# Moving the on-chip buffers of a two-layer decoder trunk to multiples of 1 KB

## The chip, the core and the metric

The kernel runs on one core of a Trainium2 chip. The metric is the device time of one execution in microseconds (us), as the median of several runs. Within a core, TensorE (PE) multiplies matrices, VectorE (DVE), ScalarE (ACT) and GpSimd (POOL) do elementwise work, and SyncE (SP) issues the transfers from the chip's main memory into SBUF, the on-chip memory of 128 partitions. A tile of SBUF is a range of bytes that is the same in every partition; its start is one address. A matmul on TensorE is two instructions: a weight load (LDWEIGHTS, shown as PEld), which reads the stationary operand of 128 columns, and the MATMUL (PE), which streams the moving operand past it, here mostly 256 columns of four bytes, into PSUM, the accumulator memory.

## The reference

Two layers on 256 tokens of width 2048, each a normalised input projection, a causal mixer, a gate and an output projection with a residual; a final RMS norm follows. All in float32.

```python
def reference(x, positions, layer_norm, mla_w_in, ..., swa_w_out, final_norm):
    for i in range(DEPTH):                       # DEPTH = 2
        h = rmsnorm(x, layer_norm[i])
        if i % 2 == 0:                           # latent attention, 16 heads, ranks 512
            y, gate = mla_mixer(h, positions, ...)
            w_out = mla_w_out[j]
        else:                                    # window 128, 32 query heads on 4 key heads, sinks
            y, gate = swa_mixer(h, positions, ...)
            w_out = swa_w_out[j]
        x = x + (y * jax.nn.silu(gate)) @ w_out
    return rmsnorm(x, final_norm)
```

## The kernel before

Activations lie transposed: 16 tiles of 128 channels by 256 tokens. Float32 values are multiplied as a rounded high part plus a low part: `hs` (layer input), `ys` (gated mixer output) and `lat` (the latent vectors `cq` and `ck`) hold the two parts side by side, 256 columns each, so a tile has 2,048 bytes per partition. Each weight piece of 1,024 columns arrives in a tile `wraw` (five buffers), ScalarE rounds it into `whi` (line 89) and VectorE writes the rest into `wlo` (line 90), four buffers each. A projection step is then three matmuls on one weight tile of 128 columns (512 bytes), written by `proj`: high weights by high input (line 250), high by low (251), low by high (252). `slab` runs eight such steps, half of the 16 that one output chunk needs.

The order is written out by hand in one function. First come the latent projections, chunk by chunk as the weights arrive. Then a loop over eight pairs of heads: queries (from `cq`), the previous pair's value products `mix` (lines 450 to 453), rotary parts, keys, values (520 to 522, where the weight piece is the moving operand and `ck` the stationary one), and four gate slabs, with the pair's scores (544 to 552) behind the first and the transposes of its probabilities (`turn`, lines 342 and 343) behind the third. The output projection of this layer follows (32 slabs on `ys`), then keys and values of the second layer. Its loop over 16 pairs of heads has, in each round, a query slab, transposes, scores (642 to 645), the second query slab, a gate slab, the value products (670 to 672) and the second gate slab. The output projection of this layer ends the kernel, its last two chunks in another order (lines 728 and 735) so that the final norm can begin early.

Tiles come from pools. A pool is one stretch of SBUF, and its tiles lie one behind the other in the order in which the code first asks for them, each rounded up to 32 bytes; the pools lie one behind the other in the order in which they are opened: `const` (everything that lives for long, with small columns such as norm factors in between), `wpool` (`wraw`, `whi`, `wlo`) and `work` (temporaries, among them small columns of 8 or 16 bytes and the three probability tiles `p`). Each small tile so shifts all that stand behind it. Adding up the sizes gives these starts, in bytes past a multiple of 512; a piece of `whi` or `wlo` is read in steps of 512 bytes and the low half of `hs` lies 1,024 behind the high half, so that the remainder holds for every matmul on the tile:

| tile | read in | before | after |
|---|---|---|---|
| `hs`, `ys`, `cq`, `ck` | projections | 96 | 0 |
| `whi`, `wlo` | projections | 416 | 0 |
| `k1s`, `vs`, `krs` | scores, values | 96 | 0 |
| `qs`, `qh`, `ql` | scores | 416 | 0 |
| `kk`, `vh`, `vl` | scores, values | 480 | 0 |
| `pth`, `ptl`, `p` | values, transposes | 160 | 0 |
| `ident` | transposes | 32 | 352 |

Modulo 1,024, the pieces of `whi` and `wlo` start at 928 and 416 by turns before, at 0 and 512 after.

Of the kernel before, what the change touches and what calls it, by code (L numbers as in the profile page):

```python
# [18 lines left out]
F32 = mybir.dt.float32  # L19
# [6 lines left out]
P = 128  # L26
D = 2048
S = 256
# [10 lines left out]
QH, KVH, HD = 32, 4, 64  # L39
# [60 lines left out]
def trunk(ctx: ExitStack, tc: tile.TileContext, a: dict):  # L100
# [3 lines left out]
    const = ctx.enter_context(tc.tile_pool(name="const", bufs=1))  # L104
    wpool = ctx.enter_context(tc.tile_pool(name="wpool", bufs=1))
    work = ctx.enter_context(tc.tile_pool(name="work", bufs=2))
    ps_p = ctx.enter_context(tc.tile_pool(name="ps_p", bufs=3, space=PSUM))
    ps_s = ctx.enter_context(tc.tile_pool(name="ps_s", bufs=2, space=PSUM))
    ps_t = ctx.enter_context(tc.tile_pool(name="ps_t", bufs=1, space=PSUM))
# [25 lines left out]
        w.add(a["w_o1"][c], D)  # L135


    first = const.tile([P, 1], F32, name="first")
    dve.memset(first, 0.0)
    act.activation(out=first, in_=first, func=AF.Sin)  # L140


    w.load(1)
    gains = const.tile([P, 3 * KC + 2 * RC], F32, name="gains")
    nc.sync.dma_start(out=gains, in_=a["gains"])
    g0, g1, gf = gains[:, 0:KC], gains[:, KC:2 * KC], gains[:, 2 * KC:3 * KC]
    gq, gkv = gains[:, 3 * KC:3 * KC + RC], gains[:, 3 * KC + RC:]
# [2 lines left out]
    def xc(c):  # L150
        return x_t[c // XQ][:, c % XQ, :]

    for j in range(XQ):
        nc.sync.dma_start(out=xc(j), in_=a["x"][0][:, j, :])
        w.load(j + 2)
    freqs = const.tile([P, 4], F32, name="freqs")
    pos_i = work.tile([P, S], I32, tag="ro3", name="pos_i")
    sinks = const.tile([P, QH], F32, name="sinks")


    ident = const.tile([P, P], F32, name="ident")
    make_identity(nc, ident)

    fold = const.tile([P, P], F32, name="fold")
    pool.memset(fold, 0.0)
    for b in (0, ROPE, -ROPE):
        pool.affine_select(out=fold, in_=fold, compare_op=ALU.not_equal, fill=1.0, base=b,
                           pattern=[[-1, P]], channel_multiplier=1)
    ones = const.tile([P, 2], F32, name="ones")
    pool.memset(ones, 1.0)  # L170
    mhalf = const.tile([P, 2], F32, name="mhalf")
    pool.memset(mhalf, -0.5)

    mask_c = const.tile([P, 2 * P], F32, name="mask_c")
    mask_w = const.tile([P, 2 * P], F32, name="mask_w")
    pool.memset(mask_c, 0.0)
    pool.memset(mask_w, 0.0)
    for m in (mask_c, mask_w):
# [8 lines left out]


    def tiny(name, n=2, bufs=2):
        return work.tile([P, n], F32, tag=name, name=name, bufs=bufs)  # L190

    def split(dst, src):

# [31 lines left out]
    def rsqrt(name, tot, n, times=None):  # L225

        e = tiny("rs_e")
        if times is None:
            dve.tensor_scalar(out=e, in0=tot, scalar1=1.0 / n, scalar2=EPS, op0=ALU.mult, op1=ALU.add)
        else:  # L230
            dve.tensor_tensor(out=e, in0=tot, in1=times, op=ALU.mult)
            dve.tensor_tensor(out=e, in0=e, in1=times, op=ALU.mult)
            dve.tensor_scalar(out=e, in0=e, scalar1=1.0 / n, scalar2=EPS, op0=ALU.mult, op1=ALU.add)
        r = const.tile([P, 2], F32, name=name)
        pool.tensor_tensor(out=r, in0=e, in1=mhalf, op=ALU.pow)
        return r

# [24 lines left out]
    def bank(pool_, tag):  # L262
        return pool_.tile([P, 512], F32, tag=tag, name=tag)
# [48 lines left out]

    def softmax(ps, j, nm, sm, mask, scale, sink):

        p = work.tile([P, 3 * P], F32, tag="p", name="p", bufs=3)
        for i in range(2):
            cols = slice(0, P) if i == 0 else slice(P, 3 * P)
            src = ps[:, 0:P] if i == 0 else ps[:, S:2 * S]
            m = mask
            if i == 0:  # L320
                m = p[:, cols]
                dve.tensor_tensor(out=m, in0=ps[:, P:S], in1=mask[:, P:], op=ALU.add)
            c = 2 * i + j
            dve.tensor_tensor_reduce(out=p[:, cols], in0=src, in1=m,  # L324
                                     scale=scale if isinstance(scale, float) else scale[:, i:i + 1],
                                     scalar=BIG if sink is None else sink, op0=ALU.add, op1=ALU.min,
                                     accum_out=nm[:, c:c + 1])
            act.activation(out=p[:, cols], in_=p[:, cols], func=AF.Exp, scale=-1.0, bias=nm[:, c:c + 1],  # L328
                           accum_out=sm[:, c:c + 1])
        return p  # L330
# [55 lines left out]
    for k in range(KC):  # L386
        if k in (1, 3, 6):
            i = (1, 3, 6).index(k) + 1
            nc.sync.dma_start(out=x_t[i], in_=a["x"][i])
        if k == 3:  # L390
            nc.sync.dma_start(out=freqs, in_=a["freqs"])
            nc.sync.dma_start(out=pos_i, in_=a["pos"].partition_broadcast(P))
            nc.sync.dma_start(out=sinks, in_=a["sinks"].partition_broadcast(P))
        split_scaled(hs[k], xc(k), g0[:, k:k + 1])
        if k == 0:
            for half in range(2):
                hi, lo = w.next()
                for ws, x in ((hi, 0), (hi, 1), (lo, 0)):
                    for c in range(RC):
                        mm(acc[half * RC + c], lhsT=ws[:, c * P:(c + 1) * P], rhs=hs[0][:, x, :],  # L400
                           start=False, stop=False)
        elif k < KC - 2:
            hi, lo = w.next()
            for c in range(2 * RC):
                n = slice(c * P, (c + 1) * P)
                proj(acc[c], (hi[:, n], lo[:, n]), hs[k], False, False)
            sq_x.add(xc(k - 1))
        elif k == KC - 1:
            last = [w.next(), w.next()]
            for j in range(KC - 3, KC):  # L410
                sq_x.add(xc(j))
            for c in range(2 * RC):
                n = slice(c * P, (c + 1) * P)
                for j, (hi, lo) in enumerate(last):
                    proj(acc[c], (hi[:, n], lo[:, n]), hs[KC - 2 + j], False, j == 1 and c % 2 == 1)
                if c % 2 == 1:
                    finish(c - 1)
                    finish(c)
        if k == 6:
            pos_f = const.tile([P, S], F32, name="pos_f")  # L420
            dve.tensor_copy(out=pos_f, in_=pos_i)
            tables = {n: rope_tables(n, i, pos_f) for i, n in enumerate(("mla", "swa"))}
    cos0, sin0 = tables["mla"]
# [37 lines left out]
    for g in range(HEADS // 2):  # L461
# [18 lines left out]
        if g == 0:  # L480
            t = bank(ps_y, "yp")
            tot = [q.total(t[:, 4 * i:4 * i + 4]) for i, q in enumerate((sq_x, sq_c["q"], sq_c["k"]))]
            r0 = rsqrt("r0", tot[0], D)

            sqc = rsqrt("sqc", tot[1], RANK, r0)
            nsq = const.tile([P, 2], F32, name="nsq")
            dve.tensor_tensor(out=nsq, in0=sqc, in1=r0, op=ALU.mult)
            dve.tensor_scalar(out=nsq, in0=nsq, scalar1=-MLA_SCALE, scalar2=None, op0=ALU.mult)
            skc = rsqrt("skc", tot[2], RANK, r0)
            sk = const.tile([P, 2], F32, name="sk")  # L490
            dve.tensor_tensor(out=sk, in0=skc, in1=r0, op=ALU.mult)
            t = bank(ps_y, "yp")
            r0B = row("r0B", r0, t[:, 0:S])
            skB = row("skB", sk, t[:, S:])
            ps = bank(ps_s, "sc")[:, 0:S]
            mm(ps, lhsT=fold, rhs=krn, start=True, stop=True)
            kr = work.tile([P, S], F32, tag="ro3", name="ro3")
            rope(kr, ps, cos0, sin0, MASK_MLA)
            dve.tensor_tensor(out=kr, in0=kr, in1=r0B, op=ALU.mult)
            split(krs, kr)  # L500
# [14 lines left out]
        for i in range(2):  # L515
            t = slice(i * P, (i + 1) * P)
            for k in range(RC):
                n = slice(k * S, (k + 1) * S)
# [77 lines left out]
    for q in range(4):  # L596
        hi, lo = w.next()
        for i in range(2):
            t = slice(i * P, (i + 1) * P)
            for k in range(4):  # L600
                kk = 4 * q + k
                n = slice(k * S, (k + 1) * S)
# [6 lines left out]
        dve.scalar_tensor_tensor(out=vs[i][:, :, 1, :], in0=v, scalar=r1[:, i:i + 1],  # L609
                                 in1=vs[i][:, :, 0, :].bitcast(F32), op0=ALU.mult, op1=ALU.subtract)  # L610

    nsink = const.tile([P, QH], F32, name="nsink")
    dve.tensor_scalar(out=nsink, in0=sinks, scalar1=-1.0, scalar2=None, op0=ALU.mult)
    qs_of, sg_of, p_of, pt_of, y_of = {}, {}, {}, {}, {}

# [107 lines left out]
    for c in tail:  # L723
        last[c] = [w.next(), w.next()]
        ps = bank(ps_p, "pp")[:, 0:S]
        for k in range(KC):
            n = slice(k % (KC // 2) * P, (k % (KC // 2) + 1) * P)
# [3 lines left out]
    def chunk(c, t):  # L731
        ps = bank(ps_p, "pp")[:, 0:S].rearrange("p (a q) -> p a q", a=2)
        for k in range(KC):
            n = slice(k % (KC // 2) * P, (k % (KC // 2) + 1) * P)
            mm(ps, lhsT=last[c][k // (KC // 2)][0][:, n], rhs=ys[k][:, :, t], start=k == 0, stop=k == KC - 1)  # L735
        xl = xc(c)[:, t]
        for n in range(2):
            dve.tensor_tensor(out=xl, in0=ps[:, n, :], in1=xl, op=ALU.add)
        sq = work.tile([P, P], F32, tag=("hx", "yg")[c % 2], name="sql", bufs=2)
        act.activation(out=sq, in_=xl, func=AF.Square)  # L740
        return sq
# [28 lines left out]
    sq = chunk(KC - 2, t1)  # L770
    r2 = norm(t0, parts)
    parts = [sq, chunk(KC - 1, t1)]
    scaled(0, t0, r2)
    scaled(1, t1, norm(t1, parts))

# [80 lines left out]
```

## Time and profile before

| | |
|---|---|
| median of three runs | 680.67 us (680.66 to 681.06) |
| the profiled execution | 684.75 us, of which the span from first to last instruction is 683.0 |
| mean granted clock of TensorE | 0.996 |
| TensorE matmuls | 667.3 us busy, 5,718 instructions |
| VectorE, ScalarE, GpSimd | 532.2, 428.0 and 66.3 us busy |

Matmuls are pipelined: several are in flight at once, so a busy TensorE says little on its own. What one matmul costs in a full stream is the distance between its start and the next one's start. The 4.08 us between the profiled execution and the median are kept apart in what follows.

### The profile page before, as it was taken

To read this page: it belongs to the slowest core of one execution; us is meant where nothing else is said; L and a number is where in the kernel's file an instruction comes from. 1 tells how busy PE (TensorE), PEld (TensorE's weight loads), DVE (VectorE), ACT (ScalarE), POOL (GpSimd) and SP (SyncE) were. 2 spreads that over 40 slices of the span, in tenths; PEclk is the share of its full clock that TensorE was granted. 3 is DMA by queue.
4 is the path that set the end of the run, shared out by engine and by line. 5 is a ranking of instruction groups with operands and counts; after the bars stand their busy time and mean duration, and the time that the engine had idled before them with its cause. 6 is when DMAs were issued, how large, how long until landed. Compare 5 with 4: busy or idle time off the path is not lost.

```text
span 683.0 us, 14550 instructions
## 1 busy us (share of the span) xinstructions
PE 667.3 (98%) x5718; PEld 663.1 (97%) x5718; DVE 532.2 (78%) x1085; ACT 428.0 (63%) x853; POOL 66.3 (10%) x72
## 2 busy tenths in 40 slices
PE   8999999999999999999999999999999999999994
PEld 7999999999999999999999999999999999999994
DVE  5897787787688686666658899998998998766664
ACT  6667656666676665444446688788778778544430
POOL 3634000000000000111110000000000000022220
PEclk9999999999999999999999999999999999999998
DMA  8664454554554555555554545545445454455604
GB/s 311 252 206 168 161 161 144 185 167 144 183 162 150 174 167 174 196 183 189 184 187 160 180 141 169 166 147 177 160 157 158 157 177 158 156 188 195 204 32 124
DMA packets 37302, 117.00 MB, mean 171 GB/s; under 512 B 4209, under 2 KB 8945, under 8 KB 37233
## 3 DMA queue, kind: packets, MB, share of 16 engines
q1 hardware_dynamic: 37232, 116.06, 51.3%
q8 instruction: 45, 0.74, 0.4%
q14 instruction: 25, 0.20, 0.1%
HBM read 113.95 MB, written 2.10 MB: 170 GB/s over the span
## 4 chain that ended last, share of the span: by engine, by line
PE 88%; DVE 4%; ACT 3%; POOL 1%; issue 1%; DMA 1%; SPq 0%; DVEq 0%; ACTq 0%; POOLq 0%
PE pp L251 24%; PE pp L250 24%; PE pp L252 24%; PE pt L342 1%; DVE wlo L90 1%; ACT whi L89 1%; PE pp L735 1%; PE pp L520 1%; PE pp L522 1%; PE pp L521 1%; PE yp L670 1%; PE pt L343 1%; DVE x L762 1%; DMA wraw<-in_w_c 1%; PE sc L642 1%
## 5 line engine op out<-in xcount | busy, mean ns | idle before, releaser
L90 DVE TENSOR_TENSOR wlo<-wraw,whi 128x1024 fp32r<-128x1024 f32 (+1 forms) x217 | 259.9, 1199 | 88.6 <-ACT whi L89 87.0
L89 ACT CAST whi<-wraw 128x1024 fp32r<-128x1024 f32 (+1 forms) x217 | 222.9, 1029 | 168.7 <-PE pp L251 142.1
L252 PE MATMUL pp<-hs,wlo 128*128 128x256 f32 x860 | 239.6, 279 | 1.3 <-DVE wlo L90 1.2
L250 PE MATMUL pp<-hs,whi 128*128 128x256 f32 x860 | 240.4, 280 | 0.4 <-ACT whi L89 0.4
L251 PE MATMUL pp<-hs,whi 128*128 128x256 f32 x860 | 239.6, 279 | 0.5 <-DVE hs L200 0.5
L252 PEld LDWEIGHTS pp<-hs,wlo 128*128 128x128 f32 x860 | 161.5, 188 | 1.9 <-DVE wlo L90 1.9
L250 PEld LDWEIGHTS pp<-hs,whi 128*128 128x128 f32 x860 | 162.6, 189 | 0.6 <-ACT whi L89 0.6
L251 PEld LDWEIGHTS pp<-hs,whi 128*128 128x128 f32 x860 | 161.6, 188 | 0.9 <-DVE hs L200 0.9
L251 PE MATMUL pp<-ys,whi 128*128 128x256 f32 x480 | 133.9, 279 | 0.1
L250 PE MATMUL pp<-ys,whi 128*128 128x256 f32 x480 | 133.9, 279 | 0.0
L252 PE MATMUL pp<-ys,wlo 128*128 128x256 f32 x480 | 133.8, 279 | 0.0
L216 POOL TENSOR_TENSOR sq_x<-sq_x,sq 128x256 f32<-128x256 f32 x43 | 53.3, 1240 | 577.2 <-ACT sq L215 335.5
L250 PEld LDWEIGHTS pp<-ys,whi 128*128 128x128 f32 x480 | 91.2, 190 | 0.0
L251 PEld LDWEIGHTS pp<-ys,whi 128*128 128x128 f32 x480 | 90.1, 188 | 0.3 <-DVE ys L195 0.3
L252 PEld LDWEIGHTS pp<-ys,wlo 128*128 128x128 f32 x480 | 90.1, 188 | 0.0
L328 ACT ACTIVATE p<-p,nm 128x128 f32<-128x128 f32 x96 | 42.7, 446 | 15.3 <-DVE nm L324 15.3
L250 PE MATMUL pp<-cq,whi 128*128 128x256 f32 x96 | 27.3, 284 | 0.0
L200 DVE SCALAR_TENSOR_TENSOR hs<-x,gains,hs 128x256 fp32r<-128x256 f32 x32 | 24.9, 790 | 2.6 <-ACT hs L199 2.6
L252 PE MATMUL pp<-cq,wlo 128*128 128x256 f32 x96 | 26.7, 278 | 0.0
L251 PE MATMUL pp<-cq,whi 128*128 128x256 f32 x96 | 26.7, 278 | 0.0
L303 DVE TENSOR_TENSOR qs<-ro,qs 64x256 fp32r<-64x256 f32 x48 | 20.2, 421 | 7.5 <-ACT qs L302 6.3
L302 ACT CAST qs<-ro 64x256 fp32r<-64x256 f32 x48 | 19.2, 400 | 8.3 <-DVE ro L296 7.7
(242 smaller groups left out, 1133.6 us busy)
## 6 DMA issues: line engine op xcount, KB each, us to landing
wraw<-in_w_g SPq DMA_DIRECT2D x64, 512.0 KB, 3.7
wraw<-in_w_o SPq DMA_DIRECT2D x64, 512.0 KB, 3.5
wraw<-in_w_q SPq DMA_DIRECT2D x32, 512.0 KB, 3.6
wraw<-in_w_ukv SPq DMA_DIRECT2D x16, 512.0 KB, 3.5
wraw<-in_w_c SPq DMA_DIRECT2D x15, 512.0 KB, 6.7
wraw<-in_w_uq SPq DMA_DIRECT2D x8, 512.0 KB, 3.6
wraw<-in_w_uq SPq DMA_DIRECT2D x8, 256.0 KB, 2.6
wraw<-in_w_k SPq DMA_DIRECT2D x4, 512.0 KB, 3.4
```

Source lines behind the costliest of these rows:

```text
L89: self.nc.scalar.copy(out=hi, in_=src)
L90: self.nc.vector.tensor_tensor(out=lo, in0=src, in1=hi.bitcast(F32), op=ALU.subtract)
L200: dve.scalar_tensor_tensor(out=dst[:, 1, :], in0=src, scalar=col, in1=dst[:, 0, :].bitcast(F32), op0=ALU.mult, op1=ALU.subtract)
L216: pool.tensor_tensor(out=self.acc, in0=self.acc, in1=t, op=ALU.add)
L250: mm(ps, lhsT=wh, rhs=rhs[:, 0, :], start=first, stop=False)
L251: mm(ps, lhsT=wh, rhs=rhs[:, 1, :], start=False, stop=False)
L252: mm(ps, lhsT=wl, rhs=rhs[:, 0, :], start=False, stop=last)
L302: act.copy(out=dst[r, j, :], in_=src[r, :])
L303: dve.tensor_tensor(out=dst[o, j, :], in0=src[r, :], in1=dst[r, j, :].bitcast(F32), op=ALU.subtract)
L328: act.activation(out=p[:, cols], in_=p[:, cols], func=AF.Exp, scale=-1.0, bias=nm[:, c:c + 1], accum_out=sm[:, c:c + 1])
L342: nc.tensor.transpose(t[:, 0, j * S + i * P:j * S + (i + 1) * P], p[:, i * P:(i + 1) * P], ident)
L343: nc.tensor.transpose(t[:, 1, j * P:(j + 1) * P], p[:, 2 * P:3 * P], ident)
```

## The change

The number of tiles, their sizes, buffers, instructions, waits and the order on each engine stay as they are. Only where the tiles lie is different. The small columns leave `const` and `work` for a pool `small`, and the probability tiles leave `work` for a pool `probs`, both opened behind `work`. In `const`, the tiles that are not multiples of 1 KB are asked for first and together, so that `x` begins at 20,480 and `hs` at 36,864; a tile `rest` that nothing uses is added as the last one of `const`, and `wpool` begins at 131,072.

```diff
     work = ctx.enter_context(tc.tile_pool(name="work", bufs=2))
+    probs = ctx.enter_context(tc.tile_pool(name="probs", bufs=3))
+    small = ctx.enter_context(tc.tile_pool(name="small", bufs=1))
...
-    first = const.tile([P, 1], F32, name="first")
+    first = small.tile([P, 1], F32, name="first")
...
     gains = const.tile([P, 3 * KC + 2 * RC], F32, name="gains")
+    ident = const.tile([P, P], F32, name="ident")
+    sinks = const.tile([P, QH], F32, name="sinks")
+    freqs = const.tile([P, 4], F32, name="freqs")
+    mask_c = const.tile([P, 2 * P], F32, name="mask_c")
+    mask_w = const.tile([P, 2 * P], F32, name="mask_w")
+    pos_f = const.tile([P, S], F32, name="pos_f")
...
-    fold = const.tile([P, P], F32, name="fold")
+    fold = small.tile([P, P], F32, name="fold")
...
     def tiny(name, n=2, bufs=2):
-        return work.tile([P, n], F32, tag=name, name=name, bufs=bufs)
+        return small.tile([P, n], F32, tag=name, name=name, bufs=bufs)
...
-        r = const.tile([P, 2], F32, name=name)
+        r = small.tile([P, 2], F32, name=name)
...
-        p = work.tile([P, 3 * P], F32, tag="p", name="p", bufs=3)
+        p = probs.tile([P, 3 * P], F32, tag="p", name="p")
...
+    const.tile([P, S], F32, name="rest")
```

In the places left out, `ones`, `mhalf`, `nsq`, `sk` and `nsink` go to `small` in the same way, and the old lines of `freqs`, `sinks`, `ident`, `mask_c`, `mask_w` and `pos_f` are taken out.

More of the change, by code (lines that the diff above doesn't have):

```diff
@@ L155, in trunk @@
         w.load(j + 2)
-    freqs = const.tile([P, 4], F32, name="freqs")
     pos_i = work.tile([P, S], I32, tag="ro3", name="pos_i")
-    sinks = const.tile([P, QH], F32, name="sinks")
-    ident = const.tile([P, P], F32, name="ident")
     make_identity(nc, ident)
-    fold = const.tile([P, P], F32, name="fold")
+    fold = small.tile([P, P], F32, name="fold")
     pool.memset(fold, 0.0)
@@ L168, in trunk @@
                            pattern=[[-1, P]], channel_multiplier=1)
-    ones = const.tile([P, 2], F32, name="ones")
+    ones = small.tile([P, 2], F32, name="ones")
     pool.memset(ones, 1.0)
-    mhalf = const.tile([P, 2], F32, name="mhalf")
+    mhalf = small.tile([P, 2], F32, name="mhalf")
     pool.memset(mhalf, -0.5)
-    mask_c = const.tile([P, 2 * P], F32, name="mask_c")
-    mask_w = const.tile([P, 2 * P], F32, name="mask_w")
     pool.memset(mask_c, 0.0)
@@ L419, in trunk @@
         if k == 6:
-            pos_f = const.tile([P, S], F32, name="pos_f")
             dve.tensor_copy(out=pos_f, in_=pos_i)
@@ L485, in trunk @@
             sqc = rsqrt("sqc", tot[1], RANK, r0)
-            nsq = const.tile([P, 2], F32, name="nsq")
+            nsq = small.tile([P, 2], F32, name="nsq")
             dve.tensor_tensor(out=nsq, in0=sqc, in1=r0, op=ALU.mult)
@@ L489, in trunk @@
             skc = rsqrt("skc", tot[2], RANK, r0)
-            sk = const.tile([P, 2], F32, name="sk")
+            sk = small.tile([P, 2], F32, name="sk")
             dve.tensor_tensor(out=sk, in0=skc, in1=r0, op=ALU.mult)
@@ L610, in trunk @@
                                  in1=vs[i][:, :, 0, :].bitcast(F32), op0=ALU.mult, op1=ALU.subtract)
-    nsink = const.tile([P, QH], F32, name="nsink")
+    nsink = small.tile([P, QH], F32, name="nsink")
     dve.tensor_scalar(out=nsink, in0=sinks, scalar1=-1.0, scalar2=None, op0=ALU.mult)
```

## The prediction

> **What bounds the kernel now.** I read the page's shares first, then the chain that ended last, then what TensorE waited for.
>
> ```profile
> span 683.0 us, 14550 instructions
> ...
> PE 667.3 (98%) x5718; PEld 663.1 (97%) x5718; DVE 532.2 (78%) x1085; ACT 428.0 (63%) x853; POOL 66.3 (10%) x72
> ...
> PE 88%; DVE 4%; ACT 3%; POOL 1%; issue 1%; DMA 1%; SPq 0%; DVEq 0%; ACTq 0%; POOLq 0%
> PE pp L251 24%; PE pp L250 24%; PE pp L252 24%; PE pt L342 1%; DVE wlo L90 1%; ACT whi L89 1%; PE pp L735 1%; PE pp L520 1%; PE pp L522 1%; PE pp L521 1%; PE yp L670 1%; PE pt L343 1%; DVE x L762 1%; DMA wraw<-in_w_c 1%; PE sc L642 1%
> ```
>
> TensorE is busy 98% of the span, and the three matmuls of a projection step, lines 250 to 252, are 72% of the chain. The list of waits has next to nothing on TensorE; its longest is the first matmul of the warm-up:
>
> ```profile
> PE pp L385 <- DVE ys L382: 1.5, 1, 1.5
> ```
>
> So the time is the number of matmuls times the distance from the start of one to the start of the next. That distance isn't printed; it comes from the first and last start of one line's instructions in a stretch. Below are such rows for line 250, which issues every third matmul of a slab: two from the first output projection (260 to 347 us), two from the second (590 to 655), and one each from two neighbouring stretches of the sliding-window layer. Columns: count, duration min/median/max in ns, first and last start in us.
>
> ```profile
> L250 PE MATMUL pp<-ys,whi x247: 281/281/281, 259.9 to 346.8; 128*128 128x256 f32 x124
> L250 PEld LDWEIGHTS pp<-ys,whi x246: 192/192/192, 260.1 to 346.7; 128*128 128x128 f32 x123
> ...
> L250 PEld LDWEIGHTS pp<-ys,whi x192: 187/188/188, 589.9 to 654.8; 128*128 128x128 f32 x192
> L250 PE MATMUL pp<-ys,whi x192: 276/276/276, 590.0 to 654.9; 128*128 128x256 f32 x192
> ...
> L250 PE MATMUL pp<-hs,whi x16: 276/276/276, 401.4 to 406.5; 128*128 128x256 f32 x16
> ...
> L250 PE MATMUL pp<-hs,whi x16: 281/281/283, 407.6 to 412.9; 128*128 128x256 f32 x16
> ```
>
> The first stretch has 246 steps of three matmuls in 86.9 us: 353.3 ns a step, 117.8 ns a matmul. The second has 191 steps in 64.9 us: 339.8 ns, 113.3 a matmul. The same code on tiles at the same addresses has two paces, 4.5 ns (3.8%) apart. In the slow one the weight load of line 250 takes 192 ns in place of 188. The last two rows show both paces within 12 us of each other (15 steps in 5.1 and in 5.3 us).
>
> **What switches the pace.** I went through the sequence of all starts. Within a run of matmuls whose operands keep their starts modulo 512 bytes the pace never changes, however long the run. All 28 switches with three equal distances on either side lie within four matmuls of a change of these starts or of a gap. One place of each direction, from the timeline (start, duration):
>
> ```profile
> 446.38 0.28 PE L670 MATMUL yp<-pth,vs 128*128 128x256 f32 x1
> ...
> 446.83 0.28 PE L672 MATMUL yp<-ptl,vs 128*128 128x256 f32 x1
> 446.95 0.28 PE L250 MATMUL pp<-hs,whi 128*128 128x256 f32 x1
> ...
> 447.54 0.28 PE L252 MATMUL pp<-hs,wlo 128*128 128x256 f32 x1
> ```
>
> From 446.38 to 446.95 there are five distances (114 ns each), from 446.95 to 447.54 again five (118 ns). The step from the value products (moving operand 160 bytes past a multiple of 512, weights 96) to a slab (moving 96, weights 416) ends the fast pace, in all 16 such places. The other direction, from the value projection of the latent layer (moving 416, weights 96) to a gate slab:
>
> ```profile
> 144.71 0.28 PE L522 MATMUL pp<-whi,ck 128*128 128x256 f32 x1
> 144.83 0.28 PE L250 MATMUL pp<-hs,whi 128*128 128x256 f32 x1
> 144.95 0.28 PE L251 MATMUL pp<-hs,whi 128*128 128x256 f32 x1
> 145.07 0.28 PE L252 MATMUL pp<-hs,wlo 128*128 128x256 f32 x1
> ...
> 145.52 0.28 PE L250 MATMUL pp<-hs,whi 128*128 128x256 f32 x1
> ```
>
> Three distances of 120, then four in 0.45 us, 113 each. And a gap: after the last matmuls of a head pair's mix the next group starts slow.
>
> ```profile
> 137.68 0.36 PE L250 MATMUL pp<-cq,whi 128*128 128x256 f32 x1
> 137.88 0.28 PE L251 MATMUL pp<-cq,whi 128*128 128x256 f32 x1
> ...
> 138.35 0.28 PE L252 MATMUL pp<-cq,wlo 128*128 128x256 f32 x1
> ```
>
> One distance of 200 ns, then four in 0.47 us, 118 each. Of the matmuls of 256 columns, 2,735 distances are at the fast pace and 2,669 at the slow one, counted over the whole trace.
>
> **The change, part by part.** Instructions, waits and queue orders stay as they are, so no term comes from a moved step. Only addresses move.
>
> 1. Operands of the projections, and with them those of scores and values, now all start 0 bytes past a multiple of 512 (and of 1 KB but for a weight piece's odd columns). The changes of start that go with the switches above vanish, and the steady pair (96, 416) becomes (0, 0). No row of the trace has this pair, so the price is bounded from both sides. Best case inside what rows show: every slow distance becomes fast, 2,669 x 4.5 ns = 12.0 us less. By stage:
>
> ```profile
> 6.00:31.80 25.80, 23.85 (x196) 22.86 (x195) 20.46 (x32) 17.72 (x32) 12.88 (x11) 1.00 0.80 310
> 257.00:391.00 134.00, 133.76 (x1133) 133.30 (x1132) 92.76 (x135) 69.80 (x111) 16.57 (x16) 1.00 0.54 180
> 401.00:575.00 174.00, 174.00 (x1514) 174.00 (x1513) 161.05 (x413) 134.85 (x316) 0.00 (x0) 1.00 0.49 162
> ```
>
> (columns: stretch, its length, then busy time of PE, PEld, DVE, ACT, POOL; clock, DMA share, GB/s.) From 257 to 391 us nearly all is slow: 3.8% of 130 is 4.9. From 401 to 575, 6.6 of every 13.1 us are slow: 3.8% of 87 is 3.3. The latent layer's loop has 708 slow distances: 3.2. The first 32 us: 0.5. Sum 11.9, the 12.0 again. Worst case inside the rows: every fast distance becomes slow, 2,735 x 4.4 = 12.0 us more. I take three quarters of the gain, 9 us, and not all of it, because the gap row (137.68) shows that a gap can start the slow pace without any change of starts, and each head pair has such gaps.
>
> 2. TensorE reads across multiples of 1 KB less often. That alone I cost at nothing: weight pieces starting 416 past a multiple of 1 KB end before the next one, those starting 928 past it cross it, and the two alternate in every slab at one pace. A moving operand of two separate 512-byte runs (line 735) costs no more than one run of 1,024 bytes; this row of the chain gives 5.44 / 48 = 113.3 ns:
>
> ```profile
> 663.80 5.44 PE pp L735 x48
> ```
>
> 3. Vector, scalar and GpSimd operands and the landing places of transfers move too. Where TensorE sets the pace this is covered: in 401 to 575 us VectorE is the busiest other engine with 161.05 of 174.00. At the fast pace the stage still needs 170.7, so VectorE, at 94%, is late next but not yet the bound. Uncovered is the start: TensorE idles 25.80 - 23.85 = 1.95 us there, and VectorE works 20.46. A gain can be no more than the 1.95; a loss of 5% on VectorE's work would be 1.0. I take 0.
>
> Sum: the profiled execution took 684.75 us, 1.75 more than its span, and 4.08 more than the median of the runs, 680.67. 684.75 - 9 = 675.7; less the 4.08, 671.7, so 672. For this case alone 668.6 (all 12.0) to 677.
>
> **The rivals.**
>
> *Slower: the slow pace becomes the rule.* Place: the gate slab behind line 522, and the one behind the scores (line 552). There a change of start brings the fast pace back today; with equal starts nothing does until a gap that happens to end fast. Price: the fast part of the latent loop (787 distances x 4.4 ns = 3.5 us) and of the sliding-window layer (822: 3.6) make 7.1, so 688; with the second output projection (743: 3.3) and the start all 12.0, 692.7. It decides where more than half of the 5,404 distances end up slow. For it: gaps before a slab mostly end slow today. Against: the long stretch from 590 us is fast on the same addresses, so nothing in a slab itself brings the slow pace back.
>
> *Nothing changes: the paces have nothing to do with addresses.* The switches sit where the code goes from one kind of product to another, so the starts change together with the PSUM bank, the shape and the waits, and the trace can't part these. Then all switches stay: 680.7. Against: where the code goes from the scores' last product to a slab (line 645 to 250), bank and tiles change but not the starts modulo 512, and in all 14 such places the pace stays. [...]
>
> *One stage gains what another loses.* If gaps go on ending as they do now, the sliding-window layer is all fast (-3.3) and the latent loop all slow (+3.5): about 681.
>
> *More than the fast pace.* The uneven starts may have a part in the 113.3 ns too. The nearest rows with a weight load of the same 128 columns are transposes, with half the moving columns:
>
> ```profile
> 452.61 0.38 PE L342 MATMUL pt<-ident,p 128*128 128x128 f32 x2
> ...
> 453.15 0.27 PE L343 MATMUL pt<-ident,p 128*128 128x128 f32 x1
> ```
>
> Five distances in 0.54 us, 108 ns. If projections came to that, 12.0 + 5,404 x 5.3 ns = 40 us less on TensorE; VectorE's 161.05 would then hold the sliding-window stage, which keeps some 2: about 642. Against: those transposes also start 32 bytes off a multiple of 64, so a wrong start alone doesn't cost time there. [...]
>
> **How the numbers follow.** Fast pace nearly everywhere, 0.37; slow pace the rule, 0.26; nothing changes, 0.23; one stage against another, 0.05; more than the fast pace, 0.09. Faster by over 0.2% (1.4 us, about what a measurement of this kernel can tell from no change): 0.37 + 0.09 + 0.01 of the fifth = 0.47. Slower: 0.26 + 0.02 = 0.28. Within: 0.25. The likeliest case gives 672. The range leaves out the deep gain (0.09) and the end of the slow case in which all 12 us are lost (0.07): 666 to 691.
>
> **What would show it.** If right: line 250's rows in 260 to 347 us have 276 and 188 ns and 339.8 ns a step; the rows behind line 672 keep 113 ns; the sliding-window stage takes 171 us in place of 174. If the slow case: steps of 353.3 ns from 590 us on too. If addresses don't matter: the same switches at the same places. My forecast fails if the gaps set the pace alone, or if (0, 0) has a pace of its own, seen as a step that is neither 340 nor 353 ns.

## The result, and the profile after

The changed kernel takes 704.81 us (four runs, 704.57 to 705.25), the kernel before 680.66 in the runs beside it (680.48 to 681.06): 1.0355 times as long, 95% interval 1.0337 to 1.0373. The forecast was 672 with a range of 666 to 691. The profiled execution took 705.25 us, 20.5 more than that of before.

The page of the changed kernel:

```profile
span 703.5 us, 14550 instructions
...
PE 690.9 (98%) x5718; PEld 686.6 (98%) x5718; DVE 534.1 (76%) x1085; ACT 429.4 (61%) x853; POOL 66.3 (9%) x72
...
PE 89%; DVE 3%; ACT 3%; POOL 2%; issue 1%; DMA 1%; SPq 0%; DVEq 0%; ACTq 0%; POOLq 0%
...
L257 PE MATMUL pp<-hs,wlo 128*128 128x256 f32 x860 | 243.8, 284 | 1.2 <-DVE wlo L90 1.0
```

TensorE has 23.6 us more of busy time with the same 5,718 matmuls; VectorE, ScalarE and GpSimd have what they had, to 2 us (534.1, 429.4 and 66.3 against 532.2, 428.0 and 66.3). The rows of single instructions hardly betray it: the one of line 257 has 284 ns, its twin before had 279.

```profile
L252 PE MATMUL pp<-hs,wlo 128*128 128x256 f32 x860 | 239.6, 279 | 1.3 <-DVE wlo L90 1.2
```

The starts do. These are rows for the first matmul of a projection step, now line 255, in the two output projections (count, duration min/median/max in ns, first and last start in us):

```profile
L255 PEld LDWEIGHTS pp<-ys,whi x242: 188/192/192, 265.9 to 352.7; 128*128 128x128 f32 x121
L255 PE MATMUL pp<-ys,whi x242: 283/283/283, 266.0 to 352.8; 128*128 128x256 f32 x121
...
L255 PE MATMUL pp<-ys,whi x181: 279/283/283, 604.8 to 669.8; 128*128 128x256 f32 x181
```

The first holds 241 steps of three matmuls in 86.8 us, 360.2 ns a step; the second 180 in 65.0, 361.1 with a stop or two. Before, they had 353.3 and 339.8. So a step is neither of the two known, and a matmul costs 120.0 ns. That holds nearly everywhere: 5,156 of 5,403 distances between matmuls of 256 columns (those under 130 ns) lie between 119 and 121. Their mean went from 115.59 to 119.89 ns, which is 23.2 us; the 84 and 85 longer ones became 1.5 us shorter in sum, and the distances behind matmuls of other widths 0.1. That makes 21.5 us between the first matmul and the last (the parts are rounded); what lies outside of them became 1.0 us shorter, and the span grew by 20.5.

The places where the pace used to switch have no switch any more. Here is the step from the value products to a gate slab, in the timeline after:

```profile
459.09 0.28 PE L676 MATMUL yp<-ptl,vs 128*128 128x256 f32 x1
459.21 0.28 PE L255 MATMUL pp<-hs,whi 128*128 128x256 f32 x1
459.33 0.28 PE L256 MATMUL pp<-hs,whi 128*128 128x256 f32 x1
459.45 0.28 PE L257 MATMUL pp<-hs,wlo 128*128 128x256 f32 x1
...
461.13 0.28 PE L256 MATMUL pp<-hs,whi 128*128 128x256 f32 x1
```

Every distance is 0.12 us, ahead of the slab and in it.

### The profile page after: what moved, and what is told of

Same layout as the page of the kernel before. It is cut to its first block, busy times and chain, and to the rows that moved or that the text cites. A ratio compares the mean times of both kernels' runs of the same rounds, so it can differ in the third digit from the quotient of the medians.

```text
span 703.5 us, 14550 instructions
## 1 busy us (share of the span) xinstructions
PE 690.9 (98%) x5718; PEld 686.6 (98%) x5718; DVE 534.1 (76%) x1085; ACT 429.4 (61%) x853; POOL 66.3 (9%) x72
## 4 chain that ended last, share of the span: by engine, by line
PE 89%; DVE 3%; ACT 3%; POOL 2%; issue 1%; DMA 1%; SPq 0%; DVEq 0%; ACTq 0%; POOLq 0%
PE pp L256 24%; PE pp L257 24%; PE pp L255 24%; PE pt L347 1%; ACT whi L89 1%; PE pp L739 1%; PE yp L674 1%; PE pp L524 1%; PE pp L526 1%; PE pp L525 1%; DMA wraw<-in_w_c 1%; DVE wlo L90 1%; POOL sq_x L221 1%; PE pt L348 1%; DVE x L766 1%
## 5 line engine op out<-in xcount | busy, mean ns | idle before, releaser
L257 PE MATMUL pp<-hs,wlo 128*128 128x256 f32 x860 | 243.8, 284 | 1.2 <-DVE wlo L90 1.0
L255 PE MATMUL pp<-hs,whi 128*128 128x256 f32 x860 | 244.3, 284 | 0.0
L256 PE MATMUL pp<-hs,whi 128*128 128x256 f32 x860 | 243.6, 283 | 0.1
L257 PEld LDWEIGHTS pp<-hs,wlo 128*128 128x128 f32 x860 | 164.8, 192 | 2.0 <-DVE wlo L90 2.0
L256 PEld LDWEIGHTS pp<-hs,whi 128*128 128x128 f32 x860 | 164.9, 192 | 0.5 <-DVE hs L205 0.4
L255 PEld LDWEIGHTS pp<-hs,whi 128*128 128x128 f32 x860 | 164.8, 192 | 0.1
L256 PE MATMUL pp<-ys,whi 128*128 128x256 f32 x480 | 135.9, 283 | 0.0
L255 PE MATMUL pp<-ys,whi 128*128 128x256 f32 x480 | 135.9, 283 | 0.0
L257 PE MATMUL pp<-ys,wlo 128*128 128x256 f32 x480 | 135.8, 283 | 0.0
L256 PEld LDWEIGHTS pp<-ys,whi 128*128 128x128 f32 x480 | 92.1, 192 | 0.2 <-DVE ys L200 0.2
L255 PEld LDWEIGHTS pp<-ys,whi 128*128 128x128 f32 x480 | 92.1, 192 | 0.0
L257 PEld LDWEIGHTS pp<-ys,wlo 128*128 128x128 f32 x480 | 92.1, 192 | 0.0
```

The costliest lines, as they stand in the source:

```text
L255: mm(ps, lhsT=wh, rhs=rhs[:, 0, :], start=first, stop=False)
L256: mm(ps, lhsT=wh, rhs=rhs[:, 1, :], start=False, stop=False)
L257: mm(ps, lhsT=wl, rhs=rhs[:, 0, :], start=False, stop=last)
```

## The experiments

Three theories. A: what counts is the difference between the start of a weight tile and the start of the moving operand, modulo some power of two; a difference of 0 is bad. B: the starts themselves count, and multiples of 64 bytes or 1 KB are bad. C: another part of the new layout does it. The tile `rest` makes the test cheap, since its size alone sets where the weight pieces begin, and with them the temporaries of `work` behind them. The kernel before ran at 680.7 us on the chip of the first measurement and at a median of 683.9 to 686.5 on those of the experiments, so ratios are taken on the same chip, and single runs are read by their traces.

All rows shown for the experiments are those of one place, the first output projection from 270 to 340 us, unless said otherwise; lines move by one or two from kernel to kernel.

**e1: the same difference on other starts.**

```diff
+    const.tile([P, 24], F32, name="shift")      # 96 bytes, ahead of gains
     gains = const.tile([P, 3 * KC + 2 * RC], F32, name="gains")
```

> Everything that TensorE reads is moved by the same 96 bytes (a tile of 96 bytes ahead of all others), so activations and weight pieces both start 96 past a multiple of 512 and none at a multiple of 64. Theory A (the pace depends on the difference between the start of the weight tile and the start of the moving operand, modulo 512; a difference of 0 costs 18 steps of 6.67 ns, 120.0 ns a matmul): the difference is still 0, so 120.0 ns everywhere and 704 to 706 us. Theory B (the starts themselves matter, multiples of 64 bytes or of 1 KB being bad): back to paces of 113 and 118 ns and about 681 us. Theory C (the order of the pools or other engines' tiles): stays at 705 too, which the other runs part from A.

Measured: 705.1 us, 1.0259 times the kernel before (1.0235 to 1.0283).

```profile
L256 PE MATMUL pp<-ys,whi x195: 283/283/283, 269.9 to 339.7; 128*128 128x256 f32 x195
```

194 steps in 69.8 us, 359.8 ns: the 120.0 ns stay. No operand is a multiple of 64 any more, so B falls.

**e2, e3, e4: other differences.** The same edit with three sizes, in bytes 320, 256 and 64:

```diff
-    const.tile([P, S], F32, name="rest")        # 1024 bytes
+    const.tile([P, 80], F32, name="rest")       # 320 bytes (64 elements: 256; 16: 64)
```

> The unused tile at the end of const has 320 bytes in place of 1024, so weight pieces start 320 past a multiple of 512 and activations at 0: the difference is that of the kernel before (416 - 96), on starts that are multiples of 64. Theory A: the two paces of before return, 113.3 and 117.8 ns, and with them 670 to 692 us. Theory B: the starts are still multiples of 64 (activations of 1 KB), so 120.0 ns and 705 us. Theory C: 705 us.

> As the last one with 256 bytes: a difference of 256, half way round. Theory A: not the 120.0 ns of a difference of 0; if the two reads collide where they come to the same place of a row of 512 bytes, the half way round is where they are farthest apart at the start, 113.3 ns or less, 670 us or less. Theories B and C: 120.0 ns, 705 us.

> As the last one with 64 bytes: a difference of 64. Theory A with a fine structure: between the paces, 113 to 120 ns; if only an exact 0 collides, below 118 ns and under 692 us. Theories B and C: 120.0 ns, 705 us.

Measured: e2 684.62 us, 0.9989 times the kernel before (0.9951 to 1.0027); e3 704.19; e4 684.4. Their rows in this order:

```profile
L255 PE MATMUL pp<-ys,whi x199: 281/281/281, 269.9 to 339.9; 128*128 128x256 f32 x199
```

```profile
L255 PE MATMUL pp<-ys,whi x195: 283/283/283, 270.1 to 339.9; 128*128 128x256 f32 x195
```

```profile
L255 PE MATMUL pp<-ys,whi x199: 281/281/282, 270.0 to 339.9; 128*128 128x256 f32 x199
```

353.5, 359.8 and 353.0 ns a step. With a difference of 320 the change costs nothing measurable, though every other part of it is still there; B and C both expected 705 us for e2 and e4 and fail there. A holds, but my modulus of 512 does not: 256 is as bad as 0, and 64 is as good as 320. What repeats is 256 bytes or less.

**e5 to e8: differences of 128, 32, 96 and 192 bytes,** by the same edit.

> Differences of 0 and 256 gave 120.0 ns, 64 and 320 two paces. Weight pieces now start 128 behind the activations (modulo 512). Theory A128 (the reads meet in a pattern that repeats every 128 bytes, as two halves of 64 bytes would): as 0 and 256, 120.0 ns, 704 to 705 us. Theory A256 (it repeats every 256 bytes, and 64 is on the way from the worst to the best): 113.3 ns or less nearly everywhere, 670 us or less.

> A difference of 32 bytes, half a step of 64. Theory A128 with whole steps of 64 bytes: the first 32 bytes of a weight tile fall into the same 64 as the moving operand's, so part of the meetings remain: between 113.3 and 120.0 ns, 680 to 705 us. Theory A256: between 0 and 64, 117 to 120 ns, 690 to 705 us. Theory A-fine (only the exact start matters, not 64-byte steps): as 64, two paces, 682 to 690 us.

> A difference of 96 bytes. Theory A128: as 32 seen from the other side (96 is 32 short of 128), the same time as e6 to 0.5%. Theory A256: better than 64, below 684 us and on the way to the time of 128.

> A difference of 192 bytes. Theory A128: as 64, the two paces of 113.3 and 117.8 ns and 681 to 690 us. Theory A256: 192 is 64 short of 256, so also as 64 unless the direction matters; then below it.

Measured: 699.04, 696.91, 698.17 and 686.03 us. Rows of e5 and e8:

```profile
L255 PE MATMUL pp<-ys,whi x197: 279/281/285, 269.9 to 339.7; 128*128 128x256 f32 x197
```

```profile
L255 PE MATMUL pp<-ys,whi x206: 276/276/276, 270.0 to 339.7; 128*128 128x256 f32 x103
```

e5 has 196 steps in 69.8 us, 356.1 ns, in place of the 360 of theory A128 and the 340 of A256; both expectations fail. e6, e7 and e8 came out as theory A128 had them (e7 within 0.2% of e6), so it is 128 itself that breaks that theory; A256 had e7 below 684 us and fails there too. e8 has 205 steps in 69.7 us, 340.0 ns: the fast pace in a stretch that was slow in e4. In the second output projection it is the other way round (from 590 to 655 us 353 ns a step in e8, 340 in e4), so the difference alone doesn't say which of the two paces comes. The mean distance between matmuls of 256 columns (those under 130 ns), over the whole trace:

| difference modulo 256 | runs | mean distance, ns | time, us |
|---|---|---|---|
| 0 | changed kernel, e1, e3, e9 | 119.9 | 704.2 to 705.2 |
| 32 | e6 | 118.2 | 696.9 |
| 64 | before, e2, e4 | 115.6 to 116.3 | 680.7 to 686.5 |
| 96 | e7 | 118.5 | 698.2 |
| 128 | e5 | 118.8 | 699.0 |
| 192 | e8 | 116.3 | 686.0 |

Differences of 64 and 192 have the two paces; 0 has one; the others have mixtures of distances from 115 to 122 ns that no longer keep one value for long. As far as tested, the pattern repeats after 256 bytes (359.8 ns a step at 0 in e1 and at 256 in e3, 353.0 at 64 in e4 and 353.5 at 320 in e2) and not after 128, since 0 and 128 differ (119.9 and 118.8 ns).

**e9: nothing of the change but the difference.** The kernel before with one unused tile:

```diff
+    const.tile([P, 48], F32, name="rest")       # 192 bytes, last of const
     scaled(0, t0, r2)
```

> The kernel before, with nothing of the change: one unused tile of 192 bytes at the end of const, so that weight pieces start 96 past a multiple of 512 as the activations do. If an equal start of weight tile and moving operand is the whole cause: 120.0 ns a matmul and 704 to 706 us, as after the change. If another part of the change counts (the pools taken apart, operands of scores and values, multiples of 64): clearly less than 704, down to 681.

Measured: 705.17 us, and in the trace:

```profile
L250 PE MATMUL pp<-ys,whi x196: 282/283/284, 269.8 to 340.0; 128*128 128x256 f32 x196
```

195 steps in 70.2 us, 360.0 ns. These 192 bytes give the whole loss, with the pools in their old order: nothing is left for theory C.

**e10: one difference for everything.** Weight pieces as in e4; in addition the moving tiles of scores and values go to a pool of their own at difference 0, in front of `wpool`, and `vs` moves to tiles of `work`, 64 bytes off:

```diff
+    mov = ctx.enter_context(tc.tile_pool(name="mov", bufs=1))
     wpool = ctx.enter_context(tc.tile_pool(name="wpool", bufs=1))
...
-        hi = work.tile([P, 6 * P], F32R, tag="pth", name="pth", bufs=1)
+        hi = mov.tile([P, 6 * P], F32R, tag="pth", name="pth", bufs=1)
...                                              # ptl, pt1 and kk likewise
-    vs = [const.tile([P, KVH, 2, HD], F32R, tag=f"latq{i}", name=f"vs{i}") for i in range(2)]
+    vs = [work.tile([P, KVH, 2, HD], F32R, tag=("qh", "ql")[i], name=f"vs{i}", bufs=1) for i in range(2)]
...
-    const.tile([P, S], F32, name="rest")
+    mov.tile([P, 16], F32, tag="rest", name="rest", bufs=1)     # 64 bytes
```

> Weight pieces 64 behind the activations (as e4), and now also the stationary tiles of scores and values (qs, qh, ql, vh, vl, v1, vs) 64 behind their moving ones (k1s, krs, kk, pth, ptl, pt1, in a pool of their own at 0). Only the value projections keep another difference (192). Theory S1 (the pace switches where the difference changes): the switch from fast to slow behind the value products of the sliding-window layer is gone, that layer is at 113.3 ns nearly throughout, 171 us from 401 to 575 in place of 174, and the time 2 to 10 us under e4's 684.4. Theory S2 (the pace switches for other reasons that stand at the same places): the same switches as in e4, 682 to 688 us.

Measured: 678.23 us, 0.9899 times the kernel before (0.9866 to 0.9932). First its row for the output projection, then one of the sliding-window layer's steps from the value products into a slab, as one row of starts:

```profile
L256 PE MATMUL pp<-ys,whi x207: 275/276/277, 269.8 to 339.9; 128*128 128x256 f32 x104
```

```profile
456.22 0.39 PE L675 MATMUL yp<-pth,vs 128*128 128x256 f32 x2
...
456.78 0.28 PE L677 MATMUL yp<-ptl,vs 128*128 128x256 f32 x1
456.90 0.28 PE L256 MATMUL pp<-hs,whi 128*128 128x256 f32 x1
...
458.14 0.28 PE L258 MATMUL pp<-hs,wlo 128*128 128x256 f32 x1
```

340.3 ns a step in the projection; in the timeline, six distances in 0.68 us up to the slab and eleven in 1.24 us inside it, 113 ns each on both sides. S1 is borne out: in 14 of the 16 places where the value products give way to a slab the distances are 112 to 115 ns on both sides, where the kernel before switched to 118 in 15 of its 16 (the two others in e10 are one round that was slow already and one that begins with a stop; the one other place of before begins with a stop too). Of 5,403 distances under 130 ns, 4,218 are at the fast pace in place of 2,735, and the mean falls from 115.59 to 114.34. Most of what is left slow, some 820 of 1,185, sits in the latent layer's loop: chiefly the 88 matmuls from the first gate slab to the transposes of each pair of heads, behind the value projection, a product that kept another difference.

**e11: a good and a bad difference within one step.** High weight tiles at 64, low ones at 0:

```diff
-    const.tile([P, S], F32, name="rest")
+    const.tile([P, 16], F32, name="rest")       # 64 bytes
...
+            if self.done == 1:
+                self.pool.tile([P, 48], F32, tag="rest2", name="rest2", bufs=1)
             lo = self.pool.tile([P, n], F32R, tag="wlo", name="wlo", bufs=self.sub_bufs)
```

> High weight tiles start 64 behind the activations (modulo 256), low ones 0. The weight load of line 257 (low) runs while the matmul of line 256 streams. If each weight load is slowed by the matmul that streams beside it: the distance from 256 to 257 is 120 ns and the two others 113 to 118, a step of three 347 to 356 ns, 685 to 695 us. If one bad pair spoils the whole pattern: 120 ns for all three and 705 us. If the pace belongs to the moving operand alone: as e4, 684 us.

Measured: 695.28 us.

```profile
L257 PE MATMUL pp<-ys,whi x199: 280/281/282, 270.0 to 340.0; 128*128 128x256 f32 x199
```

The lines of a step are 257 to 259 in this kernel. 198 steps in 70.0 us, 353.5 ns: in number what was expected if each weight load suffers from the stream beside it. But the three distances are 118 each and not one of 120 with two of 113, and e4, with no difference of 0 in its slabs, had the same 353 in this place. The second output projection tells more; here e11, then e4:

```profile
L257 PE MATMUL pp<-ys,whi x185: 280/281/282, 604.8 to 669.8; 128*128 128x256 f32 x185
```

```profile
L255 PE MATMUL pp<-ys,whi x192: 276/276/281, 589.9 to 654.9; 128*128 128x256 f32 x192
```

184 steps in 65.0 us, 353.3 ns, against 191 in 65.0, 340.3. In the whole trace of e11 some 70 distances are below 115.5 ns, in that of e4 some 2,670. So with one bad pair among the three of a step this run has lost the fast pace altogether and kept the slow one: in the slabs the loss isn't kept to one pair. (The scores and value products of e11 stand at 0 as well, so the low tiles aren't its only bad pairs, and it was run once.) In the value projections of the same run, where the low piece is the moving operand and stands at difference 0, the distance behind it has a mean of 122.0 ns (117.9 in e4, where it stands at 192) and the two others of a step 118.0 and 116.6. There the loss does sit at the pair, which speaks for the operands of TensorE itself and not for what other engines do at the time. That the weight load beside the stream is what is slowed fits this and isn't proved by it.

**e12: as e10 with 192.**

```diff
-    mov.tile([P, 16], F32, tag="rest", name="rest", bufs=1)
+    mov.tile([P, 48], F32, tag="rest", name="rest", bufs=1)     # 192 bytes
```

> As e10 with 192 in place of 64, the direction turned. S1: as e10, one constant difference in slabs, scores and values, 2 to 10 us under e8's 686.0. S2: the switches of e8, 682 to 688 us.

Measured: 688.51 us, against S1's 676 to 684. Its first output projection, then its slabs from 455 to 570 us:

```profile
L256 PE MATMUL pp<-ys,whi x207: 275/276/277, 269.9 to 339.9; 128*128 128x256 f32 x104
```

```profile
L256 PE MATMUL pp<-hs,whi x277: 278/280/281, 455.0 to 569.8; 128*128 128x256 f32 x139
```

The first is at the fast pace: 206 steps in 70.0 us, 339.8 ns. But from 412.4 to 676 us all of the 2,131 distances under 130 ns belong to the slow pace (mean 117.8), the second output projection with them, through 22 longer ones of 201 to 396 ns. So S1 is right that one constant difference takes the switches away (behind the value products the pace never changes), and wrong that this brings the fast pace. The slow one sets in with the first scores behind a round's transposes, at 412.28 us; the rounds before and after look alike, and what chose it there isn't shown.

## Why the prediction was wrong

**The step that failed** is the first of the change's parts: "No row of the trace has this pair, so the price is bounded from both sides", and then bounds taken from the two paces that the trace did have, 12 us less to 12 us more. The new pair had a pace of its own, 120.0 ns, outside both. The loss is 5,400 x 4.3 ns, twice the worst case. The prediction had named what would undo it ("if (0, 0) has a pace of its own, seen as a step that is neither 340 nor 353") but gave that no chance on the slow side; only the deep gain had one. A state that no row shows has no bound from rows that show others.

**The likeliest case** fell with it. It took the fast pace as the natural one and the slow pace as the product of unequal starts. It is the other way round: equal starts are the worst of all tried (a mean of 119.9 ns, against 118.8 for the next, 128 bytes), and the fast pace in long stretches came with a difference of 64 or 192 bytes (340.3 ns a step in e10, 340.0 in e8).

**What held.** The reading that the distance between starts is the cost, and that busy shares say nothing of it. That the pace switches where the starts change, which e10 and e12 bear out (112 to 115 ns on both sides in 14 of the 16 places in e10); what counts of the starts is their difference modulo 256 (0 and 256 both 359.8 ns a step) and not each one modulo 512, which changes none of the switches named. That crossing multiples of 1 KB costs nothing: e1 puts half of the weight pieces across one, at the same 120.0 ns. That other engines' tiles cost nothing: the row of line 90 has a mean of 1,200 ns against 1,199 before, and VectorE as a whole 534.1 us against 532.2.

**Readings that were off.** The step from the value products to a slab ends the fast pace in 15 of the 16 places and not in all: in the last one, behind stops of 445 and 221 ns near 584 us, the slab is fast. The three distances of 120 behind line 522 come from rounded starts; they are 117, 122 and 116 ns, so that row is no trace of the later 120.0. And the 0.2% taken for what a measurement can tell was too little: over all its runs the kernel before spread by 1.3%.

**The rivals.** *The slow pace becomes the rule* had the right sign and, in its mechanism, describes e12, where one constant difference kept the slow pace for 264 us; its price of 7 to 12 us was half or less of what came, and its place was wrong, since the slow pace itself vanished too. *Nothing changes* is refuted by e9, in which 192 unused bytes cost 3% (705.17 us against 685.21). The pace depends on where the weight tile starts relative to the moving operand (120.0 ns at 0 in e9; 113.3 and 117.8 at 320 in the kernel before). *One stage against another* did not occur. *More than the fast pace* has no support: in none of the 14 layouts did a long stretch go below 113.3 ns; the fastest rows, those of before from 590 us and of e12 from 270 us, have 339.8 ns a step.

## What to carry to other kernels

A round start address isn't a neutral choice when TensorE streams one tile while it loads weights from another: look at the difference of their starts, here modulo 256 bytes (a mean of 119.9 ns a matmul at 0, 115.6 to 116.3 at 64), and keep it off 0. Keeping it the same for products that follow each other gave 1% at 64 (e10, 678.23 us against 685.21) and nothing at 192 (e12, a single run, 688.51). Where TensorE is busy 98% of the time, compute the distance between starts, stage by stage; two values for the same code are a lead worth more than any share of busy time. And when a change sets up a condition that the trace has never shown, leave room beyond the trace's own extremes, on both sides.

## What the runs showed of the hardware

With 128-column weight tiles and 256 moving columns of four bytes, the distance between matmuls took three values in long stretches at differences of 0, 64 and 192 bytes: 113.3, 117.8 and 120.0 ns, which stand to each other as 51, 53 and 54. The first two are states of the same code on the same addresses, which can last for hundreds of matmuls (before, 191 steps of three at 113.3 from 590 us and 246 at 117.8 from 260 us). At difference 0 the state is nearly always the third (119 to 121 ns in 5,156 of 5,403 distances of the changed kernel), and the times hardly scatter (704.19 to 705.67 us over four layouts), while the kernel before ranged from 680.48 to 689.49 over its runs on several chips. What makes the chip choose a pace after a stop, and whether it is the weight load or the moving operand that waits, is open.
